# Modulation rows of a two-layer trunk: from multiply-adds on VectorE, ScalarE and GpSimd to products on TensorE in four column groups

## The chip, the cores and the metric

The kernel runs on one core of a Trainium2 chip. A core has TensorE (PE in the profile; PEld is its loading of weights), VectorE (DVE), ScalarE (ACT), GpSimd (POOL) and SyncE (SP, which here only issues transfers; SPq and ACTq are the queues). All are fed by semaphores, and each engine runs its own instructions in order. The metric is the time of one execution in microseconds, the median of several runs.

## The reference

Two layers over 1152 tokens (1024 latent, 128 of context) of 1024 channels. What matters here is that the two norms of a layer are modulated, by six rows of 1024 numbers that come from one conditioning vector for the latent tokens (c) and another for the context (c_ctx):

```python
silu_c, silu_ctx = jax.nn.silu(c), jax.nn.silu(c_ctx)
for l in range(2):
    mod_ctx = (silu_ctx @ w_ada[l] + b_ada[l])[None, None, :]     # w_ada[l]: 1024 x 6144, 24 MB
    mod_lat = (silu_c @ w_ada[l] + b_ada[l])[:, None, :]
    ...
    sh1, sc1, g1, sh2, sc2, g2 = jnp.split(mod, 6, axis=-1)
    h = rmsnorm(x, norm[0]) * (1.0 + sc1) + sh1
    x = x + g1 * rmsnorm(mixer(h), norm[1])
    h = rmsnorm(x, norm[2]) * (1.0 + sc2) + sh2
    f = (jax.nn.silu(h @ w_gate) * (h @ w_up)) @ w_down
    x = x + g2 * rmsnorm(f, norm[3])
```

The mixer projects h, runs retention, a Fourier mixing, latent attention (MLA) and a long convolution (Hyena, with filters that a small network gives), and projects their outputs. All is in 32-bit floats.

## The kernel before

Tokens lie in nine tiles of 128. A layer has these stages, one after another on PE: the first norm and its transposition (`norm_mod`, products named pstr); phase 1 (`phase1`: the input projection, tile acc, first for MLA and in `hu_block` for Hyena, then the long convolution, and `natural`, the rest of the columns); phase 2 (attention and retention, products sc and psr); phase 3 (output projection wo, residual, second norm); `gate_up` (products gu, Strassen's form of the gate and up projections); and the down projection (dq). A large product is three products of split operands (`mm3`, lines 129 to 131), whose weights are split on ScalarE and VectorE (hi, lo; whi and wlo in phase 1, fw in gate_up). Instructions stand on each engine in the order in which the program issues them, moved by `high_priority` blocks; a wait for a semaphore holds all that is behind it on its engine.

The modulation rows are made in three places:

- Opening, layer 0, columns 0 to 2047 (shift and scale of the first norm, in `phase1`). The weights come in 16 loads ada0 of 512 KB. For each 128 columns eight products (line 696) with silu(c) and silu(c_ctx) of a k-tile as a 128x2 weight matrix (csilu) are summed in PSUM (psada). A 32-bit product is two passes in the trace, so there are 256. Rows of 512 columns are then biased on VectorE, spread to all partitions (psrow, line 705) and copied to `rows` by ScalarE, and the nine norms take them (line 313).
- Phase 1 of layer 0, columns 2048 to 6143 (`ada_steps(0, 2 * D, 256, ...)`). A generator makes 256 columns at a time; phase 1 calls it in its loops, and each call does a step. Of each chunk eight tiles adw (128 KB each) are loaded into two buffers; VectorE multiplies each by its silu numbers (one per partition) and adds them up into two tiles adacc (lines 160 and 166). Then two products with sel, a matrix of a column of ones and one of zeros, sum over partitions into psada (line 285), and VectorE adds the bias and, for some rows, the norm's weights.
- gate_up of layer 0, all of layer 1's rows (`ada_steps(1, 0, 256, ..., (0,))`): 24 chunks; VectorE does the latent row, and for the context's ScalarE multiplies (adp, line 272) and POOL adds (line 157).

The rows go to memory (mod) and are loaded when a norm needs them. `filter_spectrum` makes the convolution's filters at the head of phase 1: the hidden rows of the small network are loaded in 9 pieces hc of 64 KB and less (two buffers), multiplied by w3 (psf, lines 391 and 399) and by a window.

Of the kernel before, what the change touches and what calls it, by code (L numbers as in the profile page):

```python
# [35 lines left out]
# ---------------------------------------------------------------- constants of the shapes  # L36
def shape_constants():
# [33 lines left out]
    # channel and position DFTs of the Fourier mixer  # L71
# [10 lines left out]
    # rotary tables, [token of the tile, tile, (first half, second half)]  # L82
# [8 lines left out]
    # retention: distances, masks (with the key scale), positions  # L91
# [7 lines left out]
# ---------------------------------------------------------------- kernel  # L99
class Kern:  # L100
    def __init__(self, ctx, tc, A):
# [6 lines left out]
        self.ident = self.cp.tile([P, P], F32, name="ident")  # L108
        nc.sync.dma_start(self.ident, A["ident"])
        self.ones = self.cp.tile([P, P], F32, name="ones")  # L110
        nc.vector.memset(self.ones, 1.0)

    # -- small helpers
# [19 lines left out]
    def rsqrt(self, y, v, pool, tag):  # L133
        """y = v ** -0.5, [p, n]"""
# [20 lines left out]
    # -- two engines for plain arithmetic  # L155
# [13 lines left out]
    # ------------------------------------------------------------ hyena: filters  # L169
    # slots of a tile spectrum (value = re - i * im)  # L170
# [3 lines left out]
    def dft_odd(self, z, d, s, y, tmp):  # L174
        """odd classes from z0, z4 ([p, 1, c]), d, s ([p, 3, c])"""
# [42 lines left out]
    def fft_class(self, r, y, ps, cons, inverse):  # L218
        """ps [p, 2, c]: (re, im) of class r; cons [p, 3, 128]: cos, sin, -sin"""
# [13 lines left out]
    def first(self, n):  # L233
        """what follows n instructions earlier"""
        return self.tc.high_priority(offset=n) if n else nullcontext()

    # ------------------------------------------------------------ modulation rows
    def load_cond(self):
# [5 lines left out]
        self.cs = self.cp.tile([P, 8, 2], F32, name="csilu")  # L244
        self.sel = self.cp.tile([P, 2, 2], F32, name="sel")
        nc.vector.memset(self.sel, 0.0)
        for i in range(2):
            nc.vector.memset(self.sel[:, i, i:i + 1], 1.0)
        csf = self.cs.rearrange("p a b -> p (a b)")
        nc.vector.scalar_tensor_tensor(out=csf, in0=th, scalar=1.0, in1=cc, op0=ALU.add, op1=ALU.mult)  # L250
        nc.vector.tensor_scalar(out=csf, in0=csf, scalar1=0.5, scalar2=None, op0=ALU.mult)
        self.mods = {(l, s): self.dram([2, D], f"mod{l}_{s}") for l in range(L) for s in range(6)}

    def ada_steps(self, l, c0, n, pool, psp, tag, dve=(0, 1)):
        """modulation rows of layer l from column c0 on, n columns at a time, as steps to do beside other work:
        w * silu(c) summed over k-tiles, then over partitions"""
        nc, A = self.nc, self.A
        for c in range(c0, 6 * D, n):
            s, hs = c // D, slice(c % D, c % D + n)
            acc = [pool.tile([P, n], F32, name=f"adacc{i}", bufs=1) for i in range(2)]  # L260
            for kt in range(8):
                w = pool.tile([P, n], F32, name="adw", bufs=2)
                nc.sync.dma_start(w, A["wada"][l, kt, :, c:c + n])
                for i in range(2):
                    cs = self.cs[:, kt, i:i + 1]
                    if i in dve and kt:
                        self.stt(acc[i], w, cs, acc[i], ALU.mult, ALU.add)
                    elif i in dve:
                        self.ts("v", acc[i], w, cs)
                    else:  # L270
                        d = acc[i] if kt == 0 else pool.tile([P, n], F32, name="adp", bufs=2)
# [1594 lines left out]
```

## Time and profile before

| | |
|---|---|
| median of three runs | 3522.32 us (3521.51 to 3538.58) |
| span of the profiled execution | 3531.2 us; no other time of that execution is recorded |
| mean granted clock of TensorE | 0.937 of full speed |
| PE / VectorE / ScalarE / POOL busy | 3206.7 / 2700.7 / 1286.5 / 1122.7 us |
| loads adw | 320 of 128 KB on SP's queue |

A row of the page's part 5, and of the view by lines, is a group: line, engine, operation, tile written <- tiles read, partitions x elements, the number of instructions, their busy time, the mean of one, and the engine's idle time just before them with what ended it. In a timeline a row is a run of instructions of one kind with its start and length. PE's products overlap, so the length of a run is less than the sum of its instructions. Where a helper issues the instruction (157: two tensors; 160: tensor times scalar, then a tensor; 120 and 125: the split), the tile's name tells what it is for.

### The profile page before, as it was taken

The numbers are of one execution on the slowest core, as the hardware profiler recorded it, in microseconds if no ns is written. First come the engines' busy times: TensorE is split into PE (matmuls) and PEld (weight loads), VectorE is DVE, ScalarE is ACT, GpSimd is POOL, SyncE is SP. The second block draws the span as 40 slices with busy tenths as digits, with TensorE's granted clock in tenths as the row PEclk, the third lists the DMA queues.
The fourth block names the chain that finished last, engine by engine and source line by source line (L and its number), as shares of the span: only waits on it lengthen the run. The fifth ranks groups of instructions, "written<-read, shape, count | busy, mean of one in ns | idle before, by whom it ended". The sixth has DMA issues, their size and how long they took to land.

```text
span 3531.2 us, 52713 instructions
## 1 busy us (share of the span) xinstructions
PE 3206.7 (91%) x18934; PEld 2830.7 (80%) x18934; DVE 2700.7 (76%) x5024; ACT 1286.5 (36%) x2496; POOL 1122.7 (32%) x947
## 2 busy tenths in 40 slices
PE   8899888999879999989968998899996999999897
PEld 5768777888779999967747787798885999998775
DVE  6676796767898888898897627666788866668898
ACT  3123113545444444443323232254544322223332
POOL 2111430001255555546661014201012422223664
PEclk8899899889989999999987999998898999999998
DMA  5454455104333344343223534531143322213223
GB/s 209 131 168 131 142 157 181 50 17 149 117 111 118 117 129 119 96 134 113 91 88 126 158 108 132 181 106 34 33 165 108 104 74 74 74 58 110 96 72 135
DMA packets 323349, 398.50 MB, mean 113 GB/s; under 512 B 60266, under 2 KB 253543, under 8 KB 322576
## 3 DMA queue, kind: packets, MB, share of 16 engines
q1 hardware_dynamic: 261312, 338.16, 30.1%
q10 hardware_dynamic: 61776, 56.97, 5.2%
q8 instruction: 150, 2.46, 0.3%
q14 instruction: 111, 0.91, 0.1%
HBM read 303.03 MB, written 92.00 MB: 112 GB/s over the span
## 4 chain that ended last, share of the span: by engine, by line
PE 55%; DVE 23%; DMA 6%; issue 6%; POOL 5%; ACT 4%; SPq 0%; ACTq 0%; DVEq 0%; POOLq 0%
PE gu L129 8%; PE gu L131 8%; PE gu L130 8%; DVE ho L125 3%; PE acc L131 3%; PE acc L130 2%; PE acc L129 2%; DMA adw<-in_wada 2%; DVE rq_w L146 2%; DVE acc L157 1%; DVE dw L125 1%; PE pstr L917 1%; DVE adacc L160 1%; POOL acc L157 1%; PE psr L1109 1%
## 5 line engine op out<-in xcount | busy, mean ns | idle before, releaser
L129 PE MATMUL dq<-dw,ho 128*128 128x512 f32 x704 | 289.3, 412 | 47.0 <-DVE acc L157 17.9
L131 PE MATMUL dq<-dw,ho 128*128 128x512 f32 x704 | 289.2, 411 | 34.9 <-DVE ho L125 34.7
L129 PE MATMUL gu<-X,fw 128*128 128x256 f32 x1024 | 290.1, 286 | 7.9 <-ACT fw L120 4.4
L160 DVE SCALAR_TENSOR_TENSOR adacc<-adw,csilu,adacc 128x256 f32<-128x256 f32 x392 | 239.7, 638 | 71.1 <-DMA adw<-in_wada 70.2
L131 PE MATMUL gu<-X,fw 128*128 128x256 f32 x1024 | 287.1, 283 | 1.8 <-DVE fw L125 1.8
L130 PE MATMUL dq<-dw,ho 128*128 128x512 f32 x704 | 287.1, 408 | 0.3 <-DVE dw L125 0.2
L130 PE MATMUL gu<-X,fw 128*128 128x256 f32 x1024 | 285.9, 282 | 0.0
L130 PE MATMUL acc<-wlo,Th 128*128 128x256 f32 (+1 forms) x720 | 217.4, 303 | 5.6 <-DVE wlo L125 5.6
L129 PE MATMUL acc<-whi,Th 128*128 128x256 f32 (+1 forms) x720 | 219.4, 307 | 0.0
L131 PE MATMUL acc<-whi,Tl 128*128 128x256 f32 (+1 forms) x720 | 215.8, 301 | 0.0
L129 PEld LDWEIGHTS dq<-dw,ho 128*128 128x128 f32 x704 | 138.2, 196 | 88.1 <-issue 41.6
L129 PEld LDWEIGHTS gu<-X,fw 128*128 128x128 f32 x1024 | 193.1, 190 | 18.6 <-ACT fw L120 8.1
L131 PEld LDWEIGHTS dq<-dw,ho 128*128 128x128 f32 x704 | 138.1, 196 | 78.3 <-DVE ho L125 45.4
L157 POOL TENSOR_TENSOR adacc<-adacc,adp 128x256 f32<-128x256 f32 x168 | 153.7, 915 | 131.4 <-ACT adp L272 124.4
L131 PEld LDWEIGHTS gu<-X,fw 128*128 128x128 f32 x1024 | 193.3, 190 | 2.3 <-DVE fw L125 2.3
L130 PEld LDWEIGHTS gu<-X,fw 128*128 128x128 f32 x1024 | 193.7, 190 | 0.0
L120 ACT ACTIVATE ho<-hraw 128x384 fp32r<-128x384 f32 (+1 forms) x192 | 87.8, 489 | 272.4 <-POOL hraw L157 254.7
L129 PE MATMUL gu<-x1s,fw 128*128 128x320 f32 x576 | 178.8, 310 | 3.6 <-DVE u L157 3.1
L131 PE MATMUL gu<-x1s,fw 128*128 128x320 f32 x576 | 179.5, 312 | 2.1 <-DVE fw L125 2.0
L130 PE MATMUL gu<-x1s,fw 128*128 128x320 f32 x576 | 179.0, 311 | 0.0
L125 DVE TENSOR_TENSOR ho<-hraw,ho 128x384 fp32r<-128x384 f32 (+1 forms) x192 | 165.6, 879 | 8.1 <-ACT ho L120 8.0
L130 PEld LDWEIGHTS dq<-dw,ho 128*128 128x128 f32 x704 | 138.3, 196 | 32.9 <-DVE dw L125 1.2
(526 smaller groups left out, 10186.7 us busy)
## 6 DMA issues: line engine op xcount, KB each, us to landing
adw<-in_wada SPq DMA_DIRECT2D x320, 128.0 KB
h<-U SPq DMA_DIRECT2D x176, 128.0 KB
X<-in_wf SPq DMA_DIRECT2D x42, 512.0 KB
fr<-in_wf SPq DMA_DIRECT2D x40, 512.0 KB
b<-in_wf SPq DMA_DIRECT2D x24, 768.0 KB
hraw<-h SPq DMA_DIRECT2D x24, 768.0 KB
pj<-pst ACTq DMA_DIRECT2D x90, 128.0 KB
G<-gt SPq DMA_DIRECT2D x36, 256.0 KB
```

The source lines that it names most:

```text
L120: nc.scalar.activation(hi, src, AF.Copy)
L125: (nc.vector if elo == "dve" else nc.gpsimd).tensor_tensor(out=lo, in0=src, in1=hi, op=ALU.subtract)
L129: mm(ps, lh, rh, start=start, stop=False)
L130: mm(ps, lh, rl, start=False, stop=False)
L131: mm(ps, ll, rh, start=False, stop=stop)
L146: nc.vector.scalar_tensor_tensor(out=w, in0=a, scalar=a[:, 0:1], in1=v, op0=ALU.mult, op1=ALU.mult)
L157: (self.nc.vector if e == "v" else self.nc.gpsimd).tensor_tensor(out=out, in0=a, in1=b, op=op)
L160: self.nc.vector.scalar_tensor_tensor(out=out, in0=a, scalar=s, in1=b, op0=op0, op1=op1)
L917: T(pst[:, j], pr[i][:, (k0 + j) * P:(k0 + j + 1) * P], self.ident)
L1109: nc.tensor.matmul(pi[:, pr], qx[q, pr, d], Sall[q, t, pr, d], start=False, stop=d == 1)
```

## The change

A chunk's eight k-tiles are no longer multiplied on VectorE, ScalarE and POOL. `ada_part` multiplies a k-tile on PE, with 32 columns of weights, into 32 of the 128 partitions of a PSUM tile: k-tile kt goes to group kt % 4, and k-tiles 4 to 7 are added to 0 to 3. The weights are a strided view of `konst`, which holds the 16 silu numbers, the identity and ones side by side: column kt and column kt + 8 are the two silu vectors, the other 30 are columns that happen to lie there. `ada_sum` copies the PSUM tile to SBUF on ScalarE and multiplies it by `sel`, which takes the two useful rows of each group and adds the four groups. The same two functions make the opening's rows. In `ada_steps` the loads are 256 KB, two k-tiles each, in two buffers: `load()` is called twice after each four products. A chunk now needs tiles adr and adc (in phase 1 one of the staging tiles). `filter_spectrum` loads the hidden rows in one transfer ha and a small one hb, into spaces hy_t and hy_d of phase 1.

```diff
-        self.ident = self.cp.tile([P, P], F32, name="ident")
+        self.konst = self.cp.tile([P, 16 + 2 * P], F32, name="konst")
+        self.ident, self.ones = self.konst[:, 16:16 + P], self.konst[:, 16 + P:]
...
+        self.sel = self.cp.tile([P, 2], F32, name="sel")
+        nc.vector.tensor_reduce(out=self.sel, in_=self.ident.rearrange("p (j i) -> p i j", j=4)[:, 0:2], axis=AX.X, op=ALU.add)
...
-    def ada_steps(self, l, c0, n, pool, psp, tag, dve=(0, 1)):
+    def ada_part(self, ps, w, kt):
+        g = 32 * (kt % 4)
+        self.nc.tensor.matmul(ps[g:g + 32], self.konst[:, kt:kt + 249:8], w, start=kt < 4, stop=kt >= 4)
+    def ada_sum(self, ps, cp, ps2):
+        self.nc.scalar.activation(cp, ps, AF.Copy)
+        self.nc.tensor.matmul(ps2, self.sel, cp, start=True, stop=True)
+    def ada_steps(self, l, c0, n, pool, psp, tag, parts, stage=None):
...
-            for kt in range(8):
-                w = pool.tile([P, n], F32, name="adw", bufs=2)
-                nc.sync.dma_start(w, A["wada"][l, kt, :, c:c + n])
-                for i in range(2):
-                    cs = self.cs[:, kt, i:i + 1]
-                    if i in dve and kt:
-                        self.stt(acc[i], w, cs, acc[i], ALU.mult, ALU.add)
...
-                        nc.scalar.activation(d, w, AF.Copy, scale=cs)
-                        if kt:
-                            self.tt("g", acc[i], acc[i], d, ALU.add)
...
+                w = pool.tile([P, 2, n], F32, name="adw", bufs=2)
+                nc.sync.dma_start(w, A["wada"][l, 2 * q:2 * q + 2, :, c:c + n].rearrange("k p c -> p k c"))
...
+        load()
+        load()
+        for i, (c, q) in enumerate(quarters):
+            if q == 0:
+                ps = psp.tile([P, n], F32, name="psada", tag=tag)
+            if q % 2 == 0:
+                continue
+            for j in range(4):
+                self.ada_part(ps, ws[i - 1 + j // 2][:, j % 2], 2 * q - 2 + j)
+            load()
+            load()
             yield
+            if q == 1:
+                continue
...
+            r = pool.tile([P, n], F32, name="adr")[:2]
+            cp = stage()[:, :n] if stage else pool.tile([P, n], F32, name="adc")
             nc.sync.dma_start(r, A["bada"][l, s:s + 1, hs].broadcast_to([2, n]))
+            ps2 = psp.tile([2, n], F32, name="psada", tag=tag)
+            self.ada_sum(ps, cp, ps2)
+            nc.vector.tensor_tensor(out=r, in0=ps2, in1=r, op=ALU.add)
+            yield
...
-            for i in range(2):
-                nc.tensor.matmul(ps, self.sel[:, i], acc[i], start=i == 0, stop=i == 1)
...
+            for _ in range(parts - 3):
+                yield
...
+        ha = p1.tile([64, 2048], F32, name="ha", tag="hy_t")
+        nc.sync.dma_start(ha, self.h2d[lo:lo + 64, 0:2048])
+        hb = p1.tile([64, P], F32, name="hb", tag="hy_d")
+        nc.sync.dma_start(hb, self.h2d[lo:lo + 64, 2048:])
         for q in range(8):
-            hc = p2.tile([64, 256], F32, name="hc", tag="hc")
-            nc.sync.dma_start(hc, self.h2d[lo:lo + 64, 256 * q:256 * q + 256])
+            hc = ha[:, 256 * q:256 * q + 256]
...
-                                nc.tensor.matmul(ps[:, j * P:j * P + P], self.cs[:, kt], w[:, kt], start=kt == 0, stop=kt == 7)
+                                self.ada_part(pa[:, j * P:j * P + P], w[:, kt], kt)
+                        ps = psp.tile([2, 512], F32, name="psada", tag="acc")
+                        self.ada_sum(pa, adp.tile([P, 512], F32, name="adc0", tag="adw", bufs=2), ps)
...
-                ada = self.ada_steps(1, 0, 256, adp, banks, "ad", (0,))
+                ada = self.ada_steps(1, 0, 256, adp, banks, "ad", 5)
```

Line numbers after the change are 1 to 19 higher. On PE, in gate_up of layer 0, this stands before between products of gate_up (x1a and X are its operands, fw its weights), once per chunk:

```order
L129 MATMUL gu<-x1a_9586,fw 128x320
L130 MATMUL gu<-x1a_9587,fw 128x320
L131 MATMUL gu<-x1a_9586,fw 128x320
L285 MATMUL psada<-adacc_9939,sel 2x256
L285 MATMUL psada<-adacc_9940,sel 2x256
L129 MATMUL gu<-X_8151,fw 128x256
L130 MATMUL gu<-X_8151,fw 128x256
L131 MATMUL gu<-X_8151,fw 128x256
```

After, at the same place, the first four k-tiles of a chunk:

```order
L130 MATMUL gu<-x1a_9299,fw 128x320
L131 MATMUL gu<-x1a_9300,fw 128x320
L132 MATMUL gu<-x1a_9299,fw 128x320
L257 MATMUL psada<-adw,konst 32x256 x4
L130 MATMUL gu<-X_7864,fw 128x256
L131 MATMUL gu<-X_7864,fw 128x256
L132 MATMUL gu<-X_7864,fw 128x256
```

and, after a second burst of four with 24 products between, and another 24, the sum of the chunk:

```order
L131 MATMUL gu<-x1s_8939,fw 128x320
L132 MATMUL gu<-x1s_8938,fw 128x320
L262 MATMUL psada<-adc,sel 2x256
L130 MATMUL gu<-X_7861,fw 128x256
L131 MATMUL gu<-X_7861,fw 128x256
```

The two products on ready sums have become nine on PE: eight on the loaded weights themselves, one on ScalarE's copy of their result.

On SP's queue in gate_up, before, the small loads of a chunk stand between the loads of k-tiles (h is gate_up's result on its way to memory):

```order
L263 DMA adw<-in_wada 128x256 x3
L280 DMA adw<-in_bada 2x256
L282 DMA adp<-in_normg 2x256
L263 DMA adw<-in_wada 128x256 x2
L290 DMA mod_4_256<-adw 2x256
L263 DMA adw<-in_wada 128x256 x3
L1425 DMA h_3_0_210<-U 128x2x128
L1425 DMA h_3_1_211<-U 128x2x128
```

After, all four loads of the chunk that follows stand in one piece, each of them waiting for PE to have read the buffer:

```order
L1444 DMA h_3_0_209<-U 128x2x128
L1444 DMA h_3_1_210<-U 128x2x128
L1444 DMA h_3_2_211<-U 128x2x128
L1444 DMA h_3_3_212<-U 128x2x128
L1444 DMA h_3_4_213<-U 128x2x64
L304 DMA mod_5_254<-adr 2x256
L295 DMA adr<-in_bada 2x256
L274 DMA adw<-in_wada 128x2x256 x4
L301 DMA adc<-in_normg 2x256
```

What has moved is the loads of weights: two of the four are needed by the second burst, and stand on the queue until the first burst has run.

On PE, at the start of layer 1's phase 1, before, the filter's products psf stand between the transpositions pstr of the nine norms:

```order
L131 MATMUL dq<-dw,ho 128x512
L391 MATMUL psf<-w_18837,hc 128x256 x3
L324 MATMUL pstr<-ident,acc_16245 128x128 x4
L391 MATMUL psf<-w_18837,hc 128x256
L324 MATMUL pstr<-ident,acc_16245 128x128 x4
L391 MATMUL psf<-w_18837,hc 128x256 x2
L324 MATMUL pstr<-ident,acc_16246 128x128 x8
L324 MATMUL pstr<-ident,acc_16247 128x128 x4
L391 MATMUL psf<-w_18837,hc 128x256 x3
L324 MATMUL pstr<-ident,acc_16247 128x128 x4
L391 MATMUL psf<-w_18837,hc 128x256
L324 MATMUL pstr<-ident,acc_16242 128x128 x8
```

After, the transpositions follow each other,

```order
L132 MATMUL dq<-dw,ho 128x512
L339 MATMUL pstr<-konst,acc_15214 128x128 x8
L339 MATMUL pstr<-konst,acc_15215 128x128 x8
L339 MATMUL pstr<-konst,acc_15216 128x128 x8
L339 MATMUL pstr<-konst,acc_15211 128x128 x8
L339 MATMUL pstr<-konst,acc_15212 128x128 x8
L339 MATMUL pstr<-konst,acc_15213 128x128 x8
L339 MATMUL pstr<-konst,acc_15217 128x128 x8
L339 MATMUL pstr<-konst,acc_15218 128x128 x8
L339 MATMUL pstr<-konst,acc_15219 128x128 x8
L130 MATMUL acc<-whi,Th_17634 128x288 x3
```

and the filter's products stand some 30 rows later, among the input projection:

```order
L130 MATMUL acc<-whi,Th_17634 128x288
L409 MATMUL psf<-w_17806,ha 128x256
L131 MATMUL acc<-wlo,Th_17634 128x288
L409 MATMUL psf<-w_17806,ha 128x256
L132 MATMUL acc<-whi,Tl_17635 128x288
L130 MATMUL acc<-whi,Th_17634 128x288
L409 MATMUL psf<-w_17806,ha 128x256
```

## Rows read from the trace of the kernel before

**Rows 1.** The page: totals; the chain by engine; VectorE's group of multiply-adds (part 5).
```profile
PE 3206.7 (91%) x18934; PEld 2830.7 (80%) x18934; DVE 2700.7 (76%) x5024; ACT 1286.5 (36%) x2496; POOL 1122.7 (32%) x947
PE 55%; DVE 23%; DMA 6%; issue 6%; POOL 5%; ACT 4%; SPq 0%; ACTq 0%; DVEq 0%; POOLq 0%
L160 DVE SCALAR_TENSOR_TENSOR adacc<-adw,csilu,adacc 128x256 f32<-128x256 f32 x392 | 239.7, 638 | 71.1 <-DMA adw<-in_wada 70.2
```

**Rows 2.** Busy time by stretch: stretch, length, busy us of each engine (instructions), clock, DMA.
```profile
130.00:356.00 226.00, 207.50 (x1018) 172.42 (x1018) 152.86 (x291) 60.31 (x108) 34.69 (x61) 0.97 0.47 146
1931.00:2132.00 201.00, 194.72 (x986) 167.56 (x985) 97.27 (x160) 59.27 (x106) 19.23 (x61) 0.99 0.42 127
357.00:596.00 239.00, 206.19 (x1269) 181.10 (x1268) 191.48 (x384) 48.99 (x112) 66.36 (x63) 0.93 0.53 164
2133.00:2350.00 217.00, 194.20 (x1264) 176.57 (x1263) 142.55 (x269) 55.40 (x135) 59.70 (x63) 0.96 0.50 153
970.00:1523.00 553.00, 527.66 (x3802) 502.72 (x3800) 485.92 (x827) 240.86 (x470) 286.59 (x267) 0.98 0.39 118
2718.00:3222.00 504.00, 495.24 (x3701) 493.33 (x3699) 334.11 (x584) 160.97 (x280) 138.75 (x103) 0.99 0.25 75
```

**Rows 3.** Timeline of PE around one burst: start, length, line, instructions [idle before].
```profile
1105.18 0.31 PE L130 MATMUL gu<-x1s,fw 128*128 128x320 f32 x1
1105.33 0.31 PE L131 MATMUL gu<-x1s,fw 128*128 128x320 f32 x1
1105.57 1.03 PE L285 MATMUL psada<-adacc,sel 128*2 128x256 f32 x4
...
1106.74 0.28 PE L130 MATMUL gu<-X,fw 128*128 128x256 f32 x1
```

**Rows 4.** Groups of PE's instructions by line and form: busy, mean ns of one, idle before.
```profile
L285 PE MATMUL psada<-adacc,sel 128*2 128x256 f32 x160 | 43.7, 386 | 5.9 <-DVE adacc L160 3.4 <-POOL adacc L157 2.0
```

**Rows 5.** Timeline of PE: products on two row groups (L1099) and on one (L1109).
```profile
640.26 0.72 PE L1099 MATMUL psr<-rqkT 64*128 64x128 f32 x8
...
645.44 0.66 PE L1109 MATMUL psr<-Sall,rqx 64*128 64x64 f32 x4
```

**Rows 6.** Timelines of PE, ScalarE and VectorE in the opening (columns as rows 3).
```profile
18.31 5.18 PE L696 MATMUL psada<-ada,csilu 128*2 128x128 f32 x46
41.68 6.28 PE L696 MATMUL psada<-ada,csilu 128*2 128x128 f32 x56
34.26 1.06 ACT L685 ACTIVATE sq<-x0a 128x1024 f32<-128x1024 f32 x1 [0.24 <-DMA x0a<-in_xs]
51.28 1.28 DVE L313 SCALAR_TENSOR_TENSOR x0a<-x0a,rs,rows 128x1024 f32<-128x1024 f32 x1 [1.91 <-ACT rows L706]
```

**Rows 7.** Busy time of instructions on adacc alone, by stretch (columns as rows 2).
```profile
130.00:356.00 226.00, 8.52 (x32) 1.68 (x32) 49.73 (x117) 0.00 (x0) 0.00 (x0) 0.97 0.47 146
357.00:596.00 239.00, 8.69 (x32) 1.87 (x32) 63.77 (x126) 0.00 (x0) 0.00 (x0) 0.93 0.53 164
970.00:1523.00 553.00, 24.47 (x92) 5.28 (x92) 138.02 (x187) 12.18 (x24) 147.26 (x163) 0.98 0.39 118
```

**Rows 8.** Waits of PE from 968 to 1535: total us, times, longest.
```profile
PE gu L129 <- DVE u L157: 16.4, 3, 12.2
```

**Rows 9.** SP's queue and ScalarE: loads and the instructions that use them; ScalarE's wait for adw.
```profile
1098.72 0.99 SPq L263 DMA_DIRECT2D adw<-in_wada  x2
1101.63 0.51 ACT L272 ACTIVATE adp<-adw,csilu 128x256 f32<-128x256 f32 x1 [1.68 <-DMA adw<-in_wada]
1888.68 1.09 SPq L598 DMA_DIRECT2D wraw<-in_winn  x2
1891.79 0.68 ACT L120 ACTIVATE whi<-wraw 128x576 fp32r<-128x576 f32 x1 [1.10 <-DMA wraw<-in_winn]
ACT adp L272 <- DMA adw<-in_wada: 146.7, 92, 4.0
```

**Rows 10.** The chain of waits from 1830 to 1900, in order of time.
```profile
1868.82 2.85 PE psf L391 x6
```

More of the change, by code (lines that the diff above doesn't have):

```diff
@@ L250, in load_cond @@
+        csf = self.cp.tile([P, 16], F32, name="csilu")
         nc.vector.scalar_tensor_tensor(out=csf, in0=th, scalar=1.0, in1=cc, op0=ALU.add, op1=ALU.mult)
[L251 removed]
+        nc.vector.tensor_scalar(out=self.konst[:, 0:16].rearrange("p (i k) -> p k i", i=2),
+                                in0=csf.rearrange("p (k i) -> p k i", i=2), scalar1=0.5, scalar2=None, op0=ALU.mult)
         self.mods = {(l, s): self.dram([2, D], f"mod{l}_{s}") for l in range(L) for s in range(6)}
[L254 to L276 removed]
@@ new lines, in ada_part, with load @@
+    def ada_part(self, ps, w, kt):
[5 more added lines that the diff above has]
+    def ada_steps(self, l, c0, n, pool, psp, tag, parts, stage=None):
+        nc, A = self.nc, self.A
+        quarters = [(c, q) for c in range(c0, 6 * D, n) for q in range(4)]
+        ws = []
+        def load():
+            if len(ws) < len(quarters):
+                c, q = quarters[len(ws)]
+                w = pool.tile([P, 2, n], F32, name="adw", bufs=2)
+                nc.sync.dma_start(w, A["wada"][l, 2 * q:2 * q + 2, :, c:c + n].rearrange("k p c -> p k c"))
+                ws.append(w)
+        load()
[12 more added lines that the diff above has]
+                continue
+            s, hs = c // D, slice(c % D, c % D + n)
+            k = {1: 0, 2: 1, 4: 2, 5: 3}.get(s)
+            r = pool.tile([P, n], F32, name="adr")[:2]
+            cp = stage()[:, :n] if stage else pool.tile([P, n], F32, name="adc")
+            nc.sync.dma_start(r, A["bada"][l, s:s + 1, hs].broadcast_to([2, n]))
+            ps2 = psp.tile([2, n], F32, name="psada", tag=tag)
+            self.ada_sum(ps, cp, ps2)
+            nc.vector.tensor_tensor(out=r, in0=ps2, in1=r, op=ALU.add)
@@ L277, in ada_steps @@
             yield
-            k = {1: 0, 2: 1, 4: 2, 5: 3}.get(s)
-            r, ng = (pool.tile([P, n], F32, name=nm, bufs=2)[:2] for nm in ("adw", "adw" if len(dve) > 1 else "adp"))
-            nc.sync.dma_start(r, A["bada"][l, s:s + 1, hs].broadcast_to([2, n]))
             if k is not None:
-                nc.sync.dma_start(ng, A["normg"][l, k:k + 1, hs].broadcast_to([2, n]))
-            ps = psp.tile([2, n], F32, name="psada", tag=tag)
-            for i in range(2):
-                nc.tensor.matmul(ps, self.sel[:, i], acc[i], start=i == 0, stop=i == 1)
@@ L286, in ada_steps @@
-            nc.vector.tensor_tensor(out=r, in0=ps, in1=r, op=ALU.add)
-            if k is not None:
-                nc.vector.scalar_tensor_tensor(out=r, in0=r, scalar=1.0 if s in (1, 4) else 0.0, in1=ng,
+                nc.sync.dma_start(cp[:2], A["normg"][l, k:k + 1, hs].broadcast_to([2, n]))
+                nc.vector.scalar_tensor_tensor(out=r, in0=r, scalar=1.0 if s in (1, 4) else 0.0, in1=cp[:2],
                                                op0=ALU.add, op1=ALU.mult)
             nc.sync.dma_start(self.mods[l, s][:, hs], r)
-            yield
+            for _ in range(parts - 3):
+                yield
@@ L691, in phase1 @@
                     for q in (0, 2, 1, 3):
-                        ps = psp.tile([2, 512], F32, name="psada", tag="acc")
+                        pa = psp.tile([P, 512], F32, name="psada", tag="acc")
                         for j in range(4):
@@ L717, in phase1 @@
             widths = [288] + [256] * 4
[L718 removed]
+            ada = self.ada_steps(0, 2 * D, 256, adp, psp, "ad", 3,
+                                  lambda: sp.tile([P, 512], F32, name="adc", tag="stg", bufs=3)) if l == 0 else iter(())
             def natural(i, kr=None):
```

13 lines of the change are left out of this document (1 added, 12 removed).

## The prediction

> **What bounds the kernel now.** I began with the page: TensorE (PE) is busy 91% of a span of 3531.2 us and VectorE 76%; the chain that ended last is 55% PE and 23% VectorE [rows 1]. What the change takes away is large in the page: 392 multiply-adds of 239.7 us on VectorE alone [rows 1]. But busy time off the chain is worth nothing, so I read it stage by stage. Layer 1 runs the same stages without modulation work beside them, so each stage has a twin, and the difference is a ceiling on what removing the old work can give [rows 2]:
> - phase 1 to the MLA and Hyena projections: 226 against 201 us, 25;
> - phase 1, the rest: 239 against 217 us, 22;
> - gate_up: 553 against 504 us, 49.
>
> Together 96 us. In gate_up PE is the wall: 527.7 of 553 us are busy, in the twin 495.2 of 504, while VectorE is at 486 and 334 [rows 2]. There, whatever goes from VectorE or POOL gives nothing, and every microsecond added to PE is a microsecond of the end. In phase 1 of layer 0 PE has holes, 18.5 and 32.8 us, where the twins have 6.3 and 22.8 [rows 2]: part of the lateness there is VectorE's.
>
> **The change part by part.** The sum is against the profiled span of 3531.2 us; the median shown is 3522.3 and the runs lie between 3521.5 and 3538.6, so the profile lies inside them, 0.25% above the median. I add the sum to the median.
>
> *What a burst on PE costs.* Before, each chunk of 256 columns ends in one burst of four passes. From the last x1s product before it (1105.33) to the second product after it (1106.74) are 1.41 us, of which the slots of the two products are 0.15 (from 1105.18 to 1105.33) and, by its columns, 0.15x256/320 = 0.12, so the burst displaces 1.14 us [rows 3]. A pass takes (1.03-0.386)/3 = 0.215 us [rows 3, 4], four 0.86; entering and leaving cost 0.28. The new sum S is one product, two passes: 2x0.215+0.28 = 0.71. The new burst B is four products, eight passes, in four column groups. If groups run at the same time it is two slots, 0.43+0.28 = 0.71; one after another, 1.72+0.28 = 2.00. No row of before has column groups. The nearest has two row groups: eight passes of 128 columns (the products of L1099) take 0.72 us, where four shorter ones on one row group take 0.66 [rows 5]. Groups overlap there, so I take 0.80 and keep both ends. A chunk is then two B and one S, 2x0.80+0.71 = 2.31 us instead of 1.14.
>
> The row groups' starts also tell the order: eight passes in 0.72 leave no room for a queue in which each pass waits for the one before it [rows 5]. The Trainium skill ("TensorE: Matmul & The Clock Gate", Part 3: Packing small matmuls) has a rule against this change: products keep program order in start and end, and only loads of weights are pulled ahead, when the row group differs; four column groups share their rows. By that rule a burst would be rival (d) below; no row of before shows column groups.
>
> *Opening.* 256 passes of 0.11 us (56 in 6.28 us) become four groups at a time [rows 6]. PE is at them from 18.3 to 48, and the first norm on VectorE starts at 51.28, when ScalarE has copied the last row [rows 6]. If they overlap, the end moves to whatever comes next: x0a lands behind the last weights, and its squares begin at 34.26 [rows 6]. Rows ready at 38 to 40 instead of 51: up to -13, but the norms after that are VectorE's and POOL's work. I take -10 (0 to -13).
>
> *Phase 1, layer 0.* The ceiling is 47. Removed: 64 passes in 16 bursts, 16x1.14 = 18 on PE, and 49.7+63.8 us of VectorE [rows 7], whose lateness is the other 29. Added: the order has 46 pieces of B (some burst is cut in two) and 16 S: 46x0.78+16x0.71 = 47. Some 14 of these should fall into holes of PE, since the twins keep 29 us of them. Against: one PSUM bank serves B, S and the next B, so PE stands while ScalarE copies and VectorE adds; VectorE's first add after a burst can be behind other work. I take 10 for this. -47+47-14+10 = -4 (-25 to +20).
>
> *gate_up, layer 0.* Removed: 24 bursts, -27; of the bursts' waits, 5.9 us in all [rows 4], some 4; of the wait of 12.2 us for u at the start [rows 8] a third, 4, since what VectorE does just before it is mostly gate_up's own splits. -35. Added: 24x2.31 = 55, 3 of it inside that start: +52. A new wait: the four loads of a chunk have two buffers, so both halves for the second B are issued only when the first B has run, and the order puts 24 products between the two, 24x0.13 = 3.2 us. A load today: issued at 1098.72, used at 1101.63, ScalarE idle for it [rows 9]; wraw, 288 KB each, issued 1888.68, used at 1891.79 [rows 9]. So 3 to 4 us against 3.2, and behind a B that waits stand all of gate_up's products: 0 to 1 us for the 18 of 24 chunks where the order is so tight, I take +6 (0 to 25). Sum +23 (+5 to +45). VectorE and POOL become free by 138 and 147 us here [rows 7]; nothing waits for that.
>
> *Filter of layer 1.* The hidden rows come in one load into a tile that is free late, so the 16 filter products leave the turn before phase 1 and go among acc. On the chain now they stand between the turns, in pieces such as 2.85 us for six passes [rows 10]; 16 products of two passes are some 15 us in that cold stretch, about 8 warm. VectorE's norms set much of that pace and the products are paid later, warm, where PE is full: -3 (-12 to +12). Layer 0's go beside the norms: 0.
>
> Sum: -10-4+23-3 = +6, so 3522+6 = 3528 us. A measurement of this kernel can't tell less than about 0.5%, 18 us, from no change: this is no change.
>
> **The rivals.**
> (a) *The second half's load decides* (slower). For: ScalarE waited 146.7 us for adw in 92 waits, up to 4.0 us, off the path [rows 9]; with the change PE waits itself, and a queue with hidden rows and weights in front makes loads later. At 1.5 us more for each of 18 chunks, 1 us for each of 16 in phase 1: 43 more, about 3570. It decides from a load of 4 us after the burst. Against: 256 KB in one load is half as many issues.
> (b) *Bursts fall into PE's holes* (faster): phase 1 gives -25, since its twins show 29 us of holes and VectorE has 113 us less; opening -12, gate_up +12 with loads in time. 3522-25-12+12-2 = 3495. Against: gate_up has no holes.
> (c) *It doesn't do what it says*: column groups run one after another. B = 2.00: 48x1.20 = 58 more in gate_up, 32 bursts x1.20 = 38 in phase 1, no gain in the opening, 10: 3528+106 = 3634. For: no row shows column groups. Against: row groups overlap.
> (d) *Half an overlap*: only the second pass of one group and the first of the next run together. B is five slots, 5x0.215+0.28 = 1.36: 48x0.56+32x0.56+5 = 50 more, 3578.
>
> **How the numbers follow.** Forecast 0.50 (its own range 3505 to 3550), (a) 0.17, (b) 0.21, (c) 0.08, (d) 0.04. The predicted time is 3528. The range 3492 to 3585 takes in (a), (d) and half of (b); outside are (c), 0.08, and what lies below 3492, some 0.09. Faster by over 0.5% is below 3505: (b) and the low edge of the forecast, 0.24. Slower, above 3540: (a), (c), (d) and 0.04 of the forecast, 0.33. The same 0.43.
>
> **What would show it.** In a B of gate_up, the eight passes: starts in fours and 0.7 to 0.8 us from product to product if groups overlap, 0.215 apart if not. PE's waits in gate_up: psada for adw, under 10 us in all, or 25 and more for (a). gate_up's window at 553+23; with (b) below 565. The norm's first instruction at about 41 instead of 51.28. In phase 1 of layer 0, PE's holes filled without new waits for PSUM. It is wrong if psada's busy time in gate_up passes 70 us, or if phase 1 comes down to its twin's 201 and 217.

## The result and the profile after

The changed kernel takes 3557.7 us, the median of 8 runs (3545.3 to 3568.9); the kernel before took 3532.9 (3521.5 to 3544.4) in 8. The ratio is 1.0074, with a 95% interval of 1.0054 to 1.0094: slower by about 26 us. The forecast was 3528 and no change, the range 3492 to 3585. The profiled execution has a span of 3557.9 us, the one before 3531.2. Cut at the first and last products of the stages, the two profiled executions compare so (us):

| stretch | before | after | difference | forecast |
|---|---|---|---|---|
| start to the end of layer 0's first acc group (opening, norms) | 130.0 | 129.4 | -0.6 | -10 |
| from there to the first wo (phases 1 and 2, layer 0) | 713.6 | 710.0 | -3.6 | -4 |
| first wo to first gu | 127.2 | 127.7 | +0.5 | 0 |
| first gu to the last dq (gate_up and down projection) | 870.7 | 886.7 | +15.9 | +23 |
| from there to the end of layer 1's first acc group | 89.4 | 103.1 | +13.7 | -3 |
| the rest of layer 1, to its last dq | 1582.1 | 1582.7 | +0.6 | 0 |

The cuts are single executions, and kernels that share a stage show how far a row moves by itself. Where gate_up is as it was (before, e5, e1), the stretch from gu to dq is 870.7, 872.4 and 875.7. The opening is 132.2 in e7, where it is as before, and 128.0, 126.9 and 131.0 in e5, e9 and e11, which share the new one. Phases 1 and 2 lie between 704.0 and 713.6 where layer 0's rows are made as before (before, e1, e5, e7, e9, e11). The rest of layer 1 lies between 1576 and 1590 over all kernels. So 5 us in a row, and 10 to 14 in the rows of phases 1 and 2 and of the rest of layer 1, are noise, and of the differences only those of gate_up and of layer 1's first acc group stand out.

The page of the changed kernel, its totals and the chain by engine, answers to [rows 1]:

```profile
PE 3244.4 (91%) x19502; PEld 2825.0 (79%) x19502; DVE 2476.5 (70%) x4574; ACT 1220.9 (34%) x2348; POOL 954.2 (27%) x779
PE 57%; DVE 24%; DMA 5%; POOL 5%; issue 5%; ACT 4%; SPq 0%; ACTq 0%; DVEq 0%; POOLq 0%
```

VectorE has lost 224 us and POOL 168, PE has gained 38, and the chain is now 57% PE. The stretches of [rows 2] after the change (length, busy us of PE, PEld, VectorE, ScalarE, POOL, granted clock, DMA), and layer 1's norms and first acc group:

```profile
130.00:397.00 267.00, 245.89 (x1222) 184.54 (x1221) 112.32 (x188) 64.12 (x122) 22.85 (x62) 0.92 0.48 145
398.00:615.00 217.00, 192.29 (x1265) 175.50 (x1264) 142.18 (x268) 56.40 (x137) 59.08 (x63) 0.95 0.51 153
967.00:1548.00 581.00, 562.91 (x4142) 513.06 (x4141) 361.69 (x647) 173.86 (x312) 143.66 (x106) 0.98 0.38 114
1854.00:1902.00 48.00, 18.58 (x73) 13.27 (x72) 43.82 (x98) 18.08 (x37) 14.09 (x6) 0.55 0.43 142
1902.00:1957.00 55.00, 53.60 (x252) 41.28 (x253) 25.34 (x22) 11.69 (x25) 1.96 (x2) 0.80 0.29 83
```

The same two stretches of layer 1 before:

```profile
1842.00:1893.00 51.00, 33.80 (x102) 22.33 (x103) 44.33 (x103) 17.40 (x36) 14.08 (x6) 0.54 0.47 153
1893.00:1931.00 38.00, 35.12 (x224) 32.65 (x223) 26.86 (x21) 12.44 (x28) 5.61 (x5) 0.90 0.30 96
```

Phase 1 of layer 0 has changed shape. Its first part takes 267 us instead of 226 and the second 217 instead of 239, which is its twin's length. The busy time of instructions on psada alone (PE, PEld, VectorE, ScalarE; POOL has none) says why:

```profile
58.00:130.00 72.00, 8.47 (x52) 2.25 (x52) 0.81 (x2) 0.79 (x2) 0.87 0.50 149
130.00:397.00 267.00, 36.29 (x236) 9.44 (x236) 5.74 (x14) 5.38 (x14) 0.92 0.48 145
398.00:615.00 217.00, 0.00 (x0) 0.00 (x0) 0.00 (x0) 0.00 (x0) 0.95 0.51 153
967.00:1548.00 581.00, 54.99 (x432) 17.08 (x432) 9.81 (x24) 9.19 (x24) 0.98 0.38 114
```

All of phase 1's modulation products, 8.5+36.3 us, run before 398; nothing is left for the second part, where before VectorE still added. The bursts, on PE in gate_up, which answer to [rows 3] (the first and the second of a chunk, and its sum):

```profile
1103.10 0.31 PE L131 MATMUL gu<-x1s,fw 128*128 128x320 f32 x1
1103.25 0.31 PE L132 MATMUL gu<-x1s,fw 128*128 128x320 f32 x1
1103.49 0.67 PE L257 MATMUL psada<-adw,konst 128*32 128x256 f32 x8
1104.09 0.39 PE L130 MATMUL gu<-X,fw 128*128 128x256 f32 x1
1104.31 0.28 PE L131 MATMUL gu<-X,fw 128*128 128x256 f32 x1
...
1107.46 0.96 PE L257 MATMUL psada<-adw,konst 128*32 128x256 f32 x8
...
1111.73 0.59 PE L262 MATMUL psada<-adc,sel 128*2 128x256 f32 x2
```

The eight passes take 0.67 us. Of the first burst, these have started up to 1103.60, 0.11 us after its start:

```profile
1103.49 0.45 PE L257 MATMUL psada<-adw,konst 128*32 128x256 f32 x4
```

A pass takes 0.215 us, so four are under way at once: the groups run together. The first group's second pass starts 0.27 us after its first one. From 1103.25 to 1104.31 are 1.06 us, less 0.15 and 0.12 for the two products' slots: 0.80, as forecast. The second burst, whose weights are loaded after the first has run, takes 0.96. A sum takes 0.59 and displaces 0.72. PE's waits in gate_up after the change, for [rows 8]:

```profile
PE gu L130 <- ACT x1s L121: 6.9, 1, 6.9
PE psada L257 <- DMA adw<-in_wada: 5.6, 5, 3.0
```

The start waits 6.9 instead of 12.2 us; the wait before dq is gone, which in the kernel before was

```profile
PE dq L129 <- DVE G L157: 9.5, 1, 9.5
```

The waits for adw that are listed are small, 5.6 us, but a burst that is cut by a late tile loses more than the listed wait: 0.96 against 0.67 without one. Reckoned as above, the 48 runs of bursts in gate_up displace 60.0 us, and 51.0 in e4 below, where the loads have more time (13 of either at the start of gate_up). The opening on PE and on VectorE (first norm of x0a, statistics ss of the last five tiles, first norm of x0b):

```profile
38.52 1.32 PE L257 MATMUL psada<-ada,konst 128*32 128x128 f32 x38
```

```profile
45.84 1.28 DVE L328 SCALAR_TENSOR_TENSOR x0a<-x0a,rs,rows 128x1024 f32<-128x1024 f32 x1 [0.54 <-ACT rows L724]
...
64.78 1.53 DVE L703 TENSOR_SCALAR ss<-ss 128x5 f32<-128x5 f32 x1 [0.35 <-ACT sq L701]
...
69.50 2.48 DVE L328 SCALAR_TENSOR_TENSOR x0b<-x0b,rs,rows 128x1024 f32<-128x1024 f32 x2
```

PE is through with the products of the rows eight us earlier than before, at 40 instead of 48, and the first norm starts at 45.84 instead of 51.28 [rows 6]. The first norm of x0b is at 69.50, where before it was at

```profile
71.25 3.15 DVE L313 SCALAR_TENSOR_TENSOR x0b<-x0b,rs,rows 128x1024 f32<-128x1024 f32 x2
```

so by x0b the 5.4 us have become 1.8. In layer 1's first acc group, the filter's products stand one or two at a time between products that PE has ready:

```profile
1921.37 0.40 PE L130 MATMUL acc<-whi,Th 128*128 128x288 f32 x1
1921.69 0.70 PE L409 MATMUL psf<-w,ha 64*128 64x256 f32 x2
1922.32 0.40 PE L131 MATMUL acc<-wlo,Th 128*128 128x288 f32 x1
1922.56 0.29 PE L132 MATMUL acc<-whi,Tl 128*128 128x288 f32 x1
1922.69 0.29 PE L130 MATMUL acc<-whi,Th 128*128 128x288 f32 x1
```

From 1921.37 to 1922.32 are 0.95 us for one filter product of two passes and one acc product, whose slot is 0.13 (1922.56 to 1922.69, the next): the filter's product displaces some 0.8 us, not the 0.5 that the forecast had for a warm one (8 us for 16).

The granted clock moves in this group too:

```profile
1910.00:1927.00 17.00, 17.00 (x78) 11.03 (x77) 5.71 (x9) 2.00 (x8) 0.00 (x0) 1.00 0.36 106
1927.00:1941.00 14.00, 14.00 (x38) 8.88 (x39) 5.49 (x5) 4.61 (x4) 0.18 (x1) 0.51 0.21 69
```

After 17 us at full speed, in which filter and acc products alternate, it is at its lower level (1.2 of 2.4 GHz) for some 14 us. In the kernel before, it is 1.00 from 1901 to the group's end at 1931.

### The profile page after: what moved, and what is told of

It reads as the page before. It is cut to its first block, busy times and chain, and to the rows that moved or that the text cites. A ratio compares the mean times of both kernels' runs of the same rounds, so it can differ in the third digit from the quotient of the medians.

```text
span 3557.9 us, 52213 instructions
## 1 busy us (share of the span) xinstructions
PE 3244.4 (91%) x19502; PEld 2825.0 (79%) x19502; DVE 2476.5 (70%) x4574; ACT 1220.9 (34%) x2348; POOL 954.2 (27%) x779
## 4 chain that ended last, share of the span: by engine, by line
PE 57%; DVE 24%; DMA 5%; POOL 5%; issue 5%; ACT 4%; SPq 0%; ACTq 0%; DVEq 0%; POOLq 0%
PE gu L130 8%; PE gu L132 8%; PE gu L131 8%; PE acc L132 3%; PE acc L130 3%; PE acc L131 3%; DVE ho L126 3%; DVE rq_w L147 2%; PE psada L257 2%; DVE acc L158 2%; DVE dw L126 1%; PE pstr L936 1%; POOL acc L158 1%; PE psr L1128 1%; PE po L953 1%
## 5 line engine op out<-in xcount | busy, mean ns | idle before, releaser
L130 PE MATMUL acc<-Th,whi 128*128 128x384 f32 x432 | 155.3, 360 | 1.4 <-ACT mst L839 1.4
L132 PE MATMUL acc<-Th,wlo 128*128 128x384 f32 x432 | 153.9, 358 | 2.1 <-DVE wlo L126 2.1
## 6 DMA issues: line engine op xcount, KB each, us to landing
h<-U SPq DMA_DIRECT2D x176, 128.0 KB
pj<-pst ACTq DMA_DIRECT2D x90, 128.0 KB
```

The costliest lines, as they stand in the source:

```text
L130: mm(ps, lh, rh, start=start, stop=False)
L132: mm(ps, ll, rh, start=False, stop=stop)
```

## The experiments

Every ratio is of timed runs against the kernel before, with its 95% interval.

**e1: before, with the hidden rows in one load.**

```diff
-            hc = p2.tile([64, 256], F32, name="hc", tag="hc")
-            nc.sync.dma_start(hc, self.h2d[lo:lo + 64, 256 * q:256 * q + 256])
+            hc = ha[:, 256 * q:256 * q + 256]     # ha, hb loaded ahead, as in the change
```

> The kernel before with only the new load of the hidden rows (ha, hb) in filter_spectrum; modulation untouched. Theory A (the filter's new place is its own cost): layer 1's stretch from the last dq to the end of the first acc group grows by what it grew with the whole change, from 89.5 to 103 us, with the psf products among acc at about 1 us each; the kernel is 10 to 17 us slower, 1.003 to 1.005 of before. Theory B (the stretch is longer only because modulation loads and their queue are in the way): no difference beyond 3 us, ratio 1.000.

1.0037 (1.0019 to 1.0055), 13 us. The stretch from the last dq to the end of the first acc group is 101.4 us. Its two parts, norms and acc group, in e1:

```profile
1840.00:1889.00 49.00, 18.68 (x74) 13.26 (x72) 43.62 (x98) 18.54 (x37) 14.08 (x6) 0.53 0.45 148
1889.00:1941.00 52.00, 51.94 (x249) 40.08 (x250) 24.96 (x22) 11.34 (x25) 1.55 (x2) 0.82 0.27 80
```

PE's busy time in the norms falls from 33.8 to 18.7 us and the norms get 2 us shorter; the acc group, full before and after, grows by 14. Theory A holds: half of the loss has nothing to do with the modulation rows. In e1, too, the clock falls again within the group: it is 0.50 from 1911 to 1924.

**e2: the changed kernel, layer 1's hidden rows in small loads.**

```diff
-            hc = ha[:, 256 * q:256 * q + 256]
+            if l == 0:
+                hc = ha[:, 256 * q:256 * q + 256]
+            else:
+                hc = p2.tile([64, 256], F32, name="hc", tag="hc")
+                nc.sync.dma_start(hc, self.h2d[lo:lo + 64, 256 * q:256 * q + 256])
```

> The changed kernel, but in layer 1 the hidden rows come in the nine small loads of before; all else as changed. Theory A: it gives back 10 to 17 us of the changed kernel's loss, so about 1.003 of before instead of 1.0074, and the psf products stand between the nine transpositions again. Theory B: nothing, 1.007.

1.0037 (1.0021 to 1.0052). The loads ha and hb stand under the same condition. The stretch is 90.6 us again, and the acc group

```profile
1902.00:1940.00 38.00, 35.11 (x217) 32.65 (x217) 27.28 (x23) 11.74 (x27) 5.17 (x5) 0.87 0.28 92
```

takes 38 us. Done from the other side, the same 13 us.

**e3: the token tiles before the first weights.** In the changed kernel one tile of x0c and x0d are issued at 54.65 and 55.16, behind weights wraw that wait for buffers; in the kernel before, all by 35.

```diff
-                with tc.high_priority(offset=450 + 350 * i if i < first else 600):
+                with tc.high_priority(offset=(450 if l else 420) + 350 * i if i < first else 600):
```

> The changed kernel with one number of the order changed: the first projection weights of layer 0 go 420 instead of 450 instructions earlier, so that all nine token tiles are loaded before them, as in the kernel before. Theory A (the opening's gain was lost because x0c and x0d are loaded behind weights that wait for buffers until 51 us): x0d is issued by 36 us, the statistics of the last five tiles are ready at about 52 instead of 65, and the first acc group ends 5 to 9 us earlier than 129.6; 5 to 9 us faster than the changed kernel, about 1.005 of before. Theory B (the norms are paced by VectorE and GpSimd, whatever comes early): the first acc group ends within 2 us of 129.6.

1.0063 (1.0042 to 1.0084), which is not to be told from 1.0074. The last tile is issued early, on SP's queue:

```profile
34.32 0.39 SPq L700 DMA_DIRECT2D x0d<-in_xp  x1
```

but VectorE comes to the statistics of the last five tiles (ss) only 2 us sooner than in the changed kernel (62.81, not the expected 52), and to x0b no sooner (71.64 against 69.50):

```profile
62.81 1.94 DVE L703 TENSOR_SCALAR ss<-ss 128x5 f32<-128x5 f32 x1
...
71.64 2.48 DVE L328 SCALAR_TENSOR_TENSOR x0b<-x0b,rs,rows 128x1024 f32<-128x1024 f32 x2
```

The first acc group ends at 129.6 as without it. Theory A of the opening falls: its gain wasn't lost in that queue.

**e4: more products between a chunk's two bursts.**

```diff
             yield
             if q == 1:
+                if parts > 3:
+                    yield
                 continue
...
-            for _ in range(parts - 3):
+            for _ in range(parts - 3 - (parts > 3)):
```

> The changed kernel, with one step of gate_up's modulation work moved, so that at least 48 instead of 24 products stand between a chunk's two bursts; nothing else. Theory A (the second half's load is late by little): the second bursts of gate_up displace 0.80 us like the first, instead of 1.05 and a few of 2 to 3 us, so gate_up is 6 to 12 us shorter, 0.997 to 0.998 of the changed kernel. Theory B (the load decides, rival a of the prediction): 20 us and more shorter. Theory C (bursts split for another reason than the load): no change, 0.80 against 1.05 stays.

1.0048 (1.0030 to 1.0066), 9 us less than the changed kernel, though the two intervals overlap. The traces are clearer: from gu to dq 878.8 us, and 880.5 in e12, which has this edit too, against 886.7, 886.3 and 888.4 in the changed kernel, e2 and e3. A second burst in e4:

```profile
1313.48 0.31 PE L132 MATMUL gu<-x1s,fw 128*128 128x320 f32 x1
1313.72 0.67 PE L257 MATMUL psada<-adw,konst 128*32 128x256 f32 x8
...
1314.54 0.28 PE L131 MATMUL gu<-X,X 128*128 128x256 f32 x1
```

0.67 us, 0.80 displaced, like a first one. The second half's load was late by little and often: Theory A.

Layer 1's filter products stand among acc in e4 as in the changed kernel, but once up the clock doesn't fall again:

```profile
1887.00:1937.00 50.00, 47.74 (x249) 37.64 (x250) 24.98 (x22) 11.46 (x25) 1.60 (x2) 0.92 0.32 90
```

The group takes 50 us there, 38 in the kernel before and 55 in the changed one. That separates what the products cost from what the clock adds; why the clock stays up in e4 isn't shown.

**e5: before, with only the opening new.** `ada_part` and `ada_sum` in the opening, with `ada_sum`'s copy in a staging tile (in e8 to e11 too); `ada_steps` and `filter_spectrum` of before.

```diff
-                                nc.tensor.matmul(ps[:, j * P:j * P + P], self.cs[:, kt], w[:, kt], start=kt == 0, stop=kt == 7)
+                                self.ada_part(pa[:, j * P:j * P + P], w[:, kt], kt)
```

> The kernel before with only the opening's rows made in four column groups; phase 1, gate_up and the filters as before. Theory A (the opening gains, and in the changed kernel modulation work of phase 1 has filled the room): the first norm starts at 45 to 47 instead of 51.28, the first acc group ends 6 to 10 us earlier than 130.1, ratio 0.997 to 0.998. Theory B (the norms are paced by VectorE and GpSimd): the first acc group ends within 2 us of 130, ratio 1.000.

0.9988 (0.9973 to 1.0003). The first norm starts at 48.01 and the first acc group ends at 128.0. PE's waits from 44 to 130 in e5 (total, times, longest):

```profile
PE pstr L383 <- POOL x0a L158: 4.5, 2, 3.8
PE pstr L383 <- DVE Tl L126: 3.8, 4, 1.6
```

PE, free earlier, waits for the norms of GpSimd and VectorE, as it did before. The opening is worth about 2 to 4 us: nearer to Theory B, not shown to differ from nothing.

**e6: one column group.**

```diff
-        g = 32 * (kt % 4)
-        self.nc.tensor.matmul(ps[g:g + 32], self.konst[:, kt:kt + 249:8], w, start=kt < 4, stop=kt >= 4)
+        self.nc.tensor.matmul(ps[:32], self.konst[:, kt:kt + 249:8], w, start=kt == 0, stop=kt == 7)
```

> The changed kernel with all eight k-tiles summed in one column group (32 columns, 32 partitions), so that no two products run at the same time; the same number of products, loads and sums. By rival c of the prediction a burst then displaces 2.0 us instead of 0.80: 48 x 1.2 = 58 us more in gate_up, about 38 more in phase 1, the opening's products back at 0.11 us a pass (8 us): 1.036 of before or more. If groups gave nothing, 1.007.

`ada_sum` then takes 32 of the 128 partitions. 1.0333 (1.0308 to 1.0358). A burst in it:

```profile
1104.00 0.31 PE L132 MATMUL gu<-x1a,fw 128*128 128x320 f32 x1
1104.24 1.94 PE L256 MATMUL psada<-adw,konst 128*32 128x256 f32 x8
...
1106.33 0.28 PE L131 MATMUL gu<-X,fw 128*128 128x256 f32 x1
```

1.94 us instead of 0.67, displaced 2.07 instead of 0.80. From gu to dq 941.5, 55 us more than the changed kernel (58 expected). The column groups do run together, and are worth some 90 us here.

**e7: before, light modulation in gate_up.** Layer 1's rows are sums over one k-tile only.

```diff
                 for i in range(2):
+                    if kt and len(dve) < 2:
+                        continue
                     cs = self.cs[:, kt, i:i + 1]
```

> The kernel before, in gate_up with the multiply-adds of seven of the eight k-tiles left out on VectorE, ScalarE and GpSimd; the loads and the bursts on TensorE stay, and layer 1's modulation rows are sums over one k-tile only. Theory A (PE is the wall in gate_up, freed VectorE time is worth only the bursts' waits and part of the start): gate_up to the first dq is 5 to 12 us shorter than 561, ratio 0.997 to 0.9985. Theory B (VectorE at 486 of 553 us held it back): 20 to 30 us shorter, ratio about 0.993.

0.9953 (0.9932 to 0.9974), 17 us; from gu to dq 852.9 instead of 870.7, between the two theories. gate_up in it, and the wait at its start:

```profile
963.00:1505.00 542.00, 524.48 (x3799) 501.04 (x3798) 369.05 (x667) 176.09 (x312) 140.74 (x106) 0.98 0.40 121
```

```profile
PE gu L129 <- ACT x1s L120: 11.3, 1, 11.3
```

VectorE is at 369 of 542 us. The start still waits 11 us, now for ScalarE; the waits of bursts (4.0 us before) are gone, and of the 9.5 us before dq some 3 are left. So freeing the three engines is worth 18 us, of which the forecast had 8.

**e8: the changed kernel with the old gate_up.** Also e2's and e3's edits.

```diff
-                ada = self.ada_steps(1, 0, 256, adp, banks, "ad", 5)
+                ada = self.ada_steps_old(1, 0, 256, adp, banks, "ad", (0,))     # the generator of before
```

> The changed kernel with layer 1's modulation rows made in gate_up as before (VectorE, ScalarE, GpSimd), the hidden rows of layer 1 in small loads as before, and the token tiles loaded before the first weights; opening and phase 1 of layer 0 as changed. If the terms add (gate_up 19, filter 13, order of loads 0 to 5): 32 to 37 us faster than the changed kernel, 0.997 to 0.999 of before. If the savings lie on the same wait and do not add: 1.002 or more.

1.0000 (0.9983 to 1.0016), between the two expectations: 26 us faster than the changed kernel, not 32 to 37. From gu to dq are 872.6 us, from there to the end of the first acc group 89.8. The losses of gate_up and of the filter are gone, and opening and phase 1 as changed give nothing that can be measured.

**e9, e10: both rows off VectorE for five chunks.** e5 and e8, and in gate_up

```diff
+            by = dve if len(dve) > 1 or 2 * n <= c < 6 * D - 3 * n else ()
...
-                    if i in dve and kt:
+                    if i in by and kt:
...
-                    elif i in dve:
+                    elif i in by:
```

> The kernel of e5 (only the opening new), and in gate_up the first two and the last three of the 24 chunks have both rows on ScalarE and GpSimd, none on VectorE. Theory A (of the 18 us that light modulation gave gate_up in e7, the start's 4 and the wait of 9.5 us before dq are VectorE's): the wait before dq falls under 3 us and gate_up to dq from 561 to about 550; ratio 0.995 to 0.997. Theory B (that wait is ScalarE's, GpSimd's or the loads'): no shorter than 559, ratio 0.999.

> The kernel of e8 (opening and phase 1 new, gate_up as before) with the same five chunks relieved. Theory A: 8 to 13 us less than e8, ratio 0.996 to 0.998. Theory B: as e8, 1.000. If new rows in phase 1 are worth anything against old ones, e10 is below e9.

1.0025 (1.0010 to 1.0040) and 1.0018 (1.0005 to 1.0031). e9 is slower than its base e5; e10's interval overlaps that of its base e8, and e9 and e10 are not to be told apart, so new rows in phase 1 are not shown to be worth anything. In e9 gate_up to the first dq is 559.0 us, but to the last dq 882.2 instead of 872.4. PE's waits there:

```profile
PE dq L130 <- DVE G L158: 8.1, 1, 8.1
PE psada L345 <- POOL adacc L158: 5.8, 6, 2.4
```

The wait of 8.1 us for G stays, only dq's first products now run before it, and bursts wait for POOL. Theory A fails: relieving VectorE at the ends by loading POOL wins nothing. Why the down projection then takes longer (323 us from its first product to its last, 309 in e5) is only in part this wait, and was not followed up.

**e11: both rows off VectorE for all chunks.** e5, and in gate_up

```diff
+            by = dve if len(dve) > 1 or False else ()     # gate_up's dve is (0,)
...
-                    if i in dve and kt:
+                    if i in by and kt:
...
-                    elif i in dve:
+                    elif i in by:
```

> The kernel of e5, and in gate_up both rows of all 24 chunks on ScalarE and GpSimd: VectorE is relieved of its 138 us there without a product more on TensorE. Theory A (18 us are VectorE's and GpSimd has room: 287 of 553 us and about 147 more): gate_up 545 to 552 us, ratio 0.994 to 0.997. Theory B (GpSimd, which prepares gate_up's weights too, becomes the wait, since each of its additions takes 0.9 us and two are needed per k-tile): gate_up 570 us and more, PE waits for fw and psada, ratio above 1.003.

1.0207 (1.0187 to 1.0228). From gu to dq 944.7 us, and PE waits for the chain of ScalarE's and POOL's pairs:

```profile
PE psada L345 <- POOL adacc L158: 48.1, 17, 7.2
```

Theory B, by a wide margin, with the wait for psada but hardly one for fw. So e7's 18 us weren't to be had by moving rows between the engines of before, in the two ways tried.

**e12: the changed kernel with the edits of e2, e3 and e4.**

```diff
+            if l == 0:                          # e2
+                hc = ha[:, 256 * q:256 * q + 256]
...
+                with tc.high_priority(offset=(450 if l else 420) + 350 * i if i < first else 600):     # e3
...
+                if parts > 3:                   # e4
+                    yield
```

> The changed kernel, all modulation on TensorE as changed, with the three repairs of order together: layer 1's hidden rows in small loads (e2), the token tiles before the first weights (e3), 48 products or more between a chunk's bursts in gate_up (e4). If the losses are separate, they add: 13+9+4 = 26 us of the changed kernel's 26, ratio 0.999 to 1.001, gate_up to the end of dq 877 to 881 us. If they are one wait seen from three sides, no better than e2 or e4 alone, 1.004.

1.0007 (0.9989 to 1.0026); from gu to dq 880.5 us, from there to the end of the first acc group 90.7. The losses are separate and add; so mended, the change neither costs nor gives anything that can be measured.

No version that makes the whole rows was faster than the kernel before beyond its interval; e5 comes nearest.

## Why the forecast was right or wrong

The measured time lies in the range, but "no change" did not come: the ratio is clear of 1, and 3557.7 us is above the 3540 from which the forecast counted as slower, with a chance of 0.33 against 0.43 for no change. The sum was +6 and +26 was measured. About 10 us of the distance from 3528 to 3557.7 are the base: it was the median of three runs, 3522.3, and eight give 3532.9. That the range held says little for the mechanism: its slow side was wide for (a) and (d), which did not come, and half of the loss is from a term that stood at -3. Of its signs, the starts in fours, the short waits for adw (5.6 us) and psada's 55 us in gate_up, under the 70 that would have spoken against it, came; the first norm was to start at 41 and started at 45.84.

*The burst.* Right in size: 0.80 forecast, 0.80 measured, the sum 0.71 and 0.72. That it fits to the hundredth is luck, since the 0.80 was taken near the low one of two ends, 0.71 and 2.00; that the groups overlap was argued, from row groups. Rival (c) is excluded by e6, and rival (d) by the same 0.67 us, since five slots would be 4x0.215+0.39 = 1.25. The trace has the four groups' first passes together, and 0.27 us later the second ones. The Trainium skill's rule of program order ("TensorE: Matmul & The Clock Gate", Part 3: Packing small matmuls) is not refuted by that, if the passes already stand in this order on PE, which the trace doesn't tell; what fell is the reading of it that a product's second pass holds up the next group's first.

*gate_up.* +23 forecast, +15.9 to the last dq (+18.8 to the first dq). Two terms were off, in opposite ways. Removed was undersized: the start and the bursts' waits came as forecast, but the wait of 9.5 us before dq was given no term, and e7 puts what the freed engines are worth at 18 us, not 8. The forecast's gate_up window ended at 1523, ahead of that wait. Added was undersized too: the load of the second half cost 8 to 9 us (e4), where 6 stood. Old bursts 27, freed engines 18, new bursts 55, late halves 8: -27-18+55+8 = +18. That PE is the wall there was right; that nothing waits for what VectorE is freed of was not.

*Rival (a)* was right in kind and too large in size: the second load is late, for 8 to 9 us in gate_up and not 27.

*Phase 1.* -4 forecast, -3.6 measured, which is no more than noise, and by another way than the terms say. The bursts came before and in its first part, and none are seen to have gone into holes (14 were booked): PE's holes in that part are 21.1 us, where they were 18.5. That part is 66 us above its twin's 201, of which 36 are busy on psada. In return the second part came down to its twin's 217, and phase 2 from 247 to 224 us. Phase 2 is not the modulation's, though: in e1, where the rows are made as before and only the hidden rows come in one load, it is as short.

```profile
596.00:843.00 247.00, 227.73 (x1414) 203.86 (x1413) 174.80 (x518) 137.67 (x296) 19.04 (x14) 0.88 0.20 61
612.00:837.00 225.00, 209.71 (x1389) 187.12 (x1388) 167.90 (x497) 133.65 (x279) 19.02 (x14) 0.93 0.22 64
```

The first row is the kernel before, the second e1, in which 26 passes of the Fourier mixing (psx) have left that stretch for an earlier place and the granted clock is higher. With the old rows and the old loads (e5, e7, e9, e11) phase 2 is 238 to 242 us. In return e1's first part is 14 us longer than before, and its second 5. So the load that the forecast put at 0 for layer 0 moved work from phase 2 into phase 1, and the whole stretch through phase 2 is 709.1 in e1, 710.0 in the changed kernel. It is a wash (e8), by the errors' cancelling as much as by the forecast.

*Opening.* -10 forecast, -0.6 measured, with modulation bursts of 8.5 us now standing before 130, and a gain of 2 to 4 by itself (e5), both within noise. The failed step is "rows ready at 38 to 40 instead of 51", taken as the end's gain: the rows were ready some 5 us sooner, but the norms behind them are paced by VectorE and GpSimd, which the forecast named as a reserve and then priced at 3 us. e3 shows that the tiles' loads were not the cause.

*Filter of layer 1.* The step that failed most: -3 forecast (-12 to +12), +13.7 measured, +13 by e1 and e2. It set the products' cold time on the chain (15 us) against their warm time (8). But on the chain between norms of VectorE's pace they cost 2 to 3 us, since PE had room there, and among acc each costs its passes and the entering and leaving, which the forecast had counted for bursts and forgot here. Two costs add up. In e4, where the clock stays up, the acc group takes 49.9 us from its first product to its last, against 37.5 before: 12.4 us for 17 products, 0.73 each. In the changed kernel it takes 54.4: the other 4.5 us (2.3 to 3.0 in e1, e3 and e6) go with the clock's second fall, some 14 us at the lower level in each of these four, for which the forecast had no term. Without this one step the forecast would have been 16 us higher, at 3544, and on the side that was measured.

## What to carry to other kernels

Moving work to the bound engine is priced by what it displaces there, entering and leaving included (some 0.3 us for each run of 32-bit products here), and against that stands what the freed engines' lateness costs, which a variant with that work left out measures in one run (e7). Every instruction that the edit moves counts: half of this loss came from a load beside the main change. A late load in front of a full engine costs more than its listed wait, and more distance in the order mends it.

## What the runs showed of the hardware

Four 32-bit products in four column groups took 0.67 us for eight passes of 256 columns, where one group took 1.94: the groups start together, pass by pass. A run of products of another shape between gate_up's costs time beside its passes of 0.215 us. With two columns of weights it was 0.28 us (two products, 1.14 for four passes) and 0.29 (one product, 0.72 for two); with 32 columns 0.35 on one group (2.07 for eight passes) and 0.37 on four (0.80 for two slots). A TensorE that is busy by its rows can lose its clock: after 17 us in which filter and acc products alternated at a granted clock of 1.00, it was 0.51 for 14 us, though in e4, with the filter products among acc as well, it was 0.92 over the whole group.
